# Delta rule: gated outputs and two gate slabs on ScalarE's DMA queue in place of SyncE's

## The chip, the cores and the metric

The kernel runs on one core of one Trainium2 chip. The metric is device time in microseconds, from the median of several executions; less is better. A core has five engines that run side by side: TensorE (PE, matmuls; PEld is its loading of weights), VectorE (DVE), ScalarE (ACT), GpSimd (POOL) and SyncE (SP). SP computes nothing here; it issues DMAs, one after the other. ScalarE can issue DMAs too, from the same instruction stream that holds its computing. A DMA that is issued is carried by the core's 16 DMA engines, and its end is told by a semaphore, on which whoever needs the data waits.

## What is computed

One step of a two-layer streaming encoder on 2048 prompt tokens and 32 sample tokens, width 1024, all in float32. The first layer is a gated delta rule with 8 heads of 128 x 128 state; the second is windowed attention. The change lies in the first layer:

```python
def delta_layer(x, conv_buf, s0, w_in, conv_w, a_log, dt_bias, norm_w, w_out, ln_g, ln_b):
    proj = x @ w_in
    qkv, new_buf = causal_conv(proj[..., :CONV_DIM], conv_buf, conv_w)
    z = proj[..., CONV_DIM:CONV_DIM + A_VW].reshape(b, l, A_HEADS, A_DV)
    ...
    o, s_new = gated_delta_rule(q, k, v, g, beta, s0.astype(jnp.float32))
    o = o * lax.rsqrt(jnp.mean(o * o, -1, keepdims=True) + RMS_EPS) * norm_w * jax.nn.silu(z.astype(jnp.float32))
    out = o.reshape(b, l, A_VW).astype(x.dtype) @ w_out
    return layer_norm(DN_ALPHA * x + out, ln_g, ln_b), new_buf, s_new.astype(x.dtype)
```

The delta rule itself runs in blocks: within a block all tokens are treated at once through the inverse of a triangular matrix, and a state `S` is handed from block to block, so the blocks follow each other.

## The kernel before

**Stages.** First `P1.qkv` projects q, k and v for all tokens and stores them to scratch memory in HBM. Then `P1.z` projects the gate z for three of five token blocks (416 tokens each), and the delta rule runs (`Delta.run`, line 775). The gate of the last two blocks is projected during the delta rule by `late_z` (L257), as filler between the matmuls of a chunk. When the filler is used up, at chunk 11 (`OPEN`), the output projection's weights are loaded (`OutNorm`, `load_part_weights`), and its tiles (`O1.tiles`) become the filler. After that the second layer follows.

**The gate slabs.** Each head's gate weights are a slab of 128 x 1024, 512 KB, loaded by `fetch_weights` (L44, its DMA is L46) into `w_raw`, then split into a high half by ScalarE (L53) and a low half (L54). `late_raw` (L251) picks the buffer: even heads use the pool `wp`, odd ones the pool of the late gate. `late_z` asks for the slab two heads ahead. Its results `z` go through two buffers (L266, L267) and are stored by SP (L268).

**The chunks.** A chunk is 128 tokens; there are 16 of them and one of the 32 sample tokens, `c0`. `load` (lines 504 and 506) brings `gb` (the decays, broadcast to all partitions), `k`, `q`, `v` and `z` in, each in two halves of four heads, all by SP. `v` and `z` share one tag with three buffers, so a half of `v` or `z` takes the buffer of the one three before it. In one round of `run` the work of several chunks is interleaved; for the chunk `ch` of the round these pieces matter here:

- `changes`: matmuls `vp` (L698) and ScalarE's copy of them (L700).
- `emit` of the chunk before, `last`: PE transposes its output (`otr`, L770), VectorE multiplies it into `z` (L771), SP stores `z` to the scratch tensor `g` (L772).
- `fade` (L619): VectorE multiplies q by the decays in `gb`; after it the buffer of `gb` is free.
- `lower` of the chunk two ahead: ScalarE's small copies (L538, L541), then VectorE's transpose (L543).
- `seen`: matmuls into the one bank `op` (L712, L716) and ScalarE's copy to `o` (L718), in two halves; the second half needs the bank that the copy of the first has emptied. `squares` (L744) follows on ScalarE.
- `turn_v`: PE transposes the halves of `v` (`vtr`, L583).

**Order.** PE, VectorE and ScalarE run the delta rule in the order in which the code writes it down. The order on SP and GpSimd is chosen by the program's scheduler, from its own simulated times. On every queue an instruction waits until its semaphores are reached, and what is behind it waits too.

Of the kernel before, what the change touches and what calls it, by code (L numbers as in the profile page):

```python
# [40 lines left out]
    return es.enter_context(tc.tile_pool(name=name, bufs=bufs, **kw))  # L41


def fetch_weights(nc, pool, src):  # L44
    raw = pool.tile([128, KC, 128], F32, tag="w_raw", name="w_raw", bufs=1)
    nc.sync.dma_start(raw[:], src)  # L46
    return raw


# [8 lines left out]
def split_weights(nc, pool, src, sub):  # L58

    return split_fetched(nc, pool, fetch_weights(nc, pool, src), sub)  # L60
# [30 lines left out]
def drain(gen):  # L91
    for _ in gen:
        pass


class P1:
# [131 lines left out]
    def z(self, blocks, pool, tags, ps, sub, w):  # L228

        nc = self.nc  # L230
        for h in range(8):
            self.fetched = fetch_weights(nc, self.wp, self.I["w_in"][25 + h]) if h < 7 else None
            self.next, self.sub = None, sub
            for b in blocks:
                p = ps()
                yield from project(nc, p[:, :TB], w, self.x[b])
                th = pool.tile([128, TB], F32, tag=tags[0], name="zth")
                z = pool.tile([128, TB], F32, tag=tags[1], name="z")
                nc.scalar.activation(th[:], p[:, :TB], AF.Tanh, scale=0.5)
                nc.vector.tensor_scalar(out=z[:], in0=p[:, :TB], scalar1=self.nwh[:, 0:1], scalar2=None, op0=ALU.mult)  # L240
                nc.vector.scalar_tensor_tensor(out=z[:], in0=th[:], scalar=1.0, in1=z[:], op0=ALU.add, op1=ALU.mult)
                nc.sync.dma_start(self.T["z"][h, :, b * TB:(b + 1) * TB], z[:])
                self.split()
            w = self.next
# [6 lines left out]
    def late_raw(self, pool, h):  # L251

        if h % 2 == 0:
            return fetch_weights(self.nc, self.wp, self.I["w_in"][24 + h])
        return fetch_weights(self.nc, pool, self.I["w_in"][24 + h])

    def late_z(self, pool, w, raw):  # L257

# [174 lines left out]
class Delta:  # L433
# [329 lines left out]
    def emit(self, ch):  # L763

        nc, V, T, n = self.nc, self.nc.vector, self.T, ch.n
        for q in range(2):
            z = ch.z[q]
            tr = self.pc.tile([128, 4, 128], F32, tag="sc", name="otr")
            for j in range(4):
                nc.tensor.transpose(tr[:, j, :n], ch.o[:n, q * 4 + j, :], self.G["ident"][:n, :n])  # L770
            V.tensor_tensor(out=z[:, :, :n], in0=tr[:, :, :n], in1=z[:, :, :n], op=ALU.mult)  # L771
            nc.sync.dma_start(T["g"][q * 4:q * 4 + 4, :, ch.t0:ch.t0 + n].rearrange("h p t -> p h t"), z[:, :, :n])  # L772
            yield

    def run(self, chunks, S, first, second, side, done):


        V, P = self.nc.vector, self.nc.gpsimd
        none = iter(())
        at = lambda i: chunks[i] if 0 <= i < len(chunks) else None  # L780
        gen = lambda f, c, *a: f(c, *a) if c else none

        def go(*gens):
            for g in gens:
                next(g, None)

        c0, c1, c2 = chunks[:3]
        for name in ("gb", "k", "q", "v"):
            self.load(c1, name)
        for name in ("gb", "k", "q"):  # L790
            self.load(c2, name)
        fill = first.give
        drain(self.decays(c0))
        side(False)
        fill(9.0)
        side(False)
        low = self.lower(c0)
        go(low, low)
        fill(1.0)
        k, w, g, d, low = self.turn_k(c0), self.turn_v(c0), self.inside(c0), self.decays(c1), self.lower(c1)  # L800
        for s, us in ((w, 0.6), (k, 0.6), (w, 0.6), (k, 0.6), (g, 0.6), (g, 0.6), (d, 0.0), (d, 0.0), (d, 1.2), (d, 1.2),
                      (low, 1.2), (low, 1.2)):
            go(s)
            fill(us)
        drain(self.powers(c0))
        drain(self.fade(c0))
        side(False)
        self.spread(c0)
        k, w, g = self.turn_k(c1), self.turn_v(c1), self.inside(c1)
        for s, us in ((k, 1.0), (w, 1.0), (k, 1.0), (w, 1.0), (g, 1.0), (g, 1.0)):  # L810
            go(s)
            fill(us)
        drain(self.powers(c1))
        drain(self.decays(c2))
        self.S, S = S, self.S
        e, seen = self.errors(c0), self.seen(c0)
        go(e, e, seen)
        last, z, x = None, none, self.fade(c1)
        go(x)
        for i in range(len(chunks) + 1):  # L820
            ch, nx, n2, n3 = at(i), at(i + 1), at(i + 2), at(i + 3)
            if i == self.OPEN:
                first.rest()
            more, gate = 0.0 if n2 else 1.0, 1.13 if i < self.OPEN else 0.0
            if not n2:
                fill = second.give
            vp, a, sq, t = (gen(f, c) for f, c in ((self.changes, ch), (self.advance, ch), (self.squares, ch),
                                                   (lambda c: self.chain(c, V, c.split, 31), nx)))
            low = gen(self.lower, n2)
            go(low, x, low)  # L830
            if n2:
                self.load(n2, "v", (0,))
            go(vp, vp, z, z, x, x, low, low, t)
            if n2:
                drain(self.chain(n2, P, 0, n2.split))
            if n3:
                self.load(n3, "gb")
            if last:
                done(last)
            fill(2 * more)  # L840
            go(seen, a, t, a, t)
            fill(more)
            go(sq, seen)
            if i > self.OPEN:
                side(True)
            if n2:
                self.load(n2, "v", (1,))
            if n3:
                self.load(n3, "q", (0,))
            if i == self.OPEN:  # L850
                side(None)
                side(True)
            go(a, t, a, t, seen, sq)
            side(False)
            fill(2 * more + gate)
            if i + 4 == len(chunks):
                next(second.gen)
            if i + 2 == len(chunks):
                c0.o = self.four.tile([128, 8, 128], F32, tag="gb", name="os", bufs=2)
                self.nc.sync.dma_start(c0.o[:NS], self.T["o"][:, :, :])  # L860
            if not ch:
                self.load(c0, "z")
                drain(self.emit(c0))
                done(c0)
                break
            if i == 0:
                self.save("s_delta")
                self.S = S
            k, w, g, e, v, r, o = (gen(f, c) for f, c in (
                (self.turn_k, n2), (self.turn_v, n2), (self.inside, n2), (self.errors, nx), (self.invert, nx),  # L870
                (self.norms, ch), (self.scale, ch)))
            go(e, t, t)
            drain(t)
            if nx:
                self.spread(nx)
            go(w, e)
            if n3:
                self.load(n3, "k")
            go(g)
            fill(2 * more + 2 * gate)  # L880
            d = gen(self.decays, n3)
            p = gen(self.powers, n2)
            go(v)
            fill(gate)
            go(r, r, r, g, r, r, v, r, k, r, d)
            if i > self.OPEN:
                side(True)
            if i == 14:
                side(True)
                side(True)  # L890
            go(v, r, v)
            if i:
                self.load(ch, "z")
            fill(more)
            seen = gen(self.seen, nx)
            go(w, r, p, r, seen, k, r, d, r)
            if n3:
                self.load(n3, "q", (1,))
            fill(more)
            drain(r)  # L900
            go(o)
            if not nx:
                go(o)
                fill(2.0)
            fill(more)
            go(v, o, d)
            if i + 3 == len(chunks):
                next(second.gen)
            if i:
                z = self.emit(ch)  # L910
            else:
                self.nc.sync.dma_start(self.T["o"][:, :, :], ch.o[:NS])
            x = gen(self.fade, n2)
            go(x)
            fill(more)
            last = ch if i else None
        self.save("p_delta")
# [861 lines left out]
```

## Time and profile before

| what | value |
|---|---|
| time of three runs | 2275.78, 2281.08, 2286.36 us; median 2281.08 |
| profiled execution | 2287.22 us, its span 2285.4 us |
| PE busy | 2198.2 us, 96% of the span |
| VectorE, ScalarE, GpSimd busy | 1390.5, 896.5, 838.5 us |
| bytes moved by DMA | 257.70 MB, mean 113 GB/s |
| by SP's queue (q1) | 240.45 MB, 36.6% of the DMA engines' time |
| by ScalarE's queue (q10) | 14.91 MB, 2.0% |
| delta rule's stores of `g`, first and last | at 803.7 and 1226.0 us |

In the timeline a row has the start, the duration, the engine, the line, the operation and the tiles (out<-in); a bracket at the end tells how long the engine had been idle before and what ended that. `SPq` and `ACTq` are instructions of the queue itself, which issue or wait; their duration is the time to issue, not the transfer. In the list of waits of SP's queue the numbers are total, count and longest. The chain of waits is followed back from the last instruction; a row of it with "DMA" has the time from the issue to the moment at which the waiting work went on, as far as it lies on the chain. The row of a window has its bounds and length, the busy time of PE, PEld, VectorE, ScalarE and GpSimd with counts, the granted PE clock, the DMA engines' busy share and GB/s.

### The profile page before, as it was taken

How to read it: one execution, taken by the hardware profiler on the slowest of the kernel's cores; microseconds unless marked ns; L12 is line 12 of the kernel's file. 1: busy time of each engine (PE TensorE's matmuls, PEld its weight loads, DVE VectorE, ACT ScalarE, POOL GpSimd, SP SyncE). 2: the span in 40 equal slices, each digit the busy share in tenths (PEclk: the TensorE clock that was granted, in tenths of full speed). 3: DMA queues.
4: the chain of work that ended last, by engine and by line, in shares of the span. 5: the costliest groups of instructions: out<-in, count | busy, mean ns of one | idle time of the engine just before them, and what ended most of it. 6: DMA issues, size and time to landing. Idle time of an engine off the chain costs nothing.

```text
span 2285.4 us, 36741 instructions
## 1 busy us (share of the span) xinstructions
PE 2198.2 (96%) x13810; PEld 2007.0 (88%) x13810; DVE 1390.5 (61%) x2705; ACT 896.5 (39%) x2222; POOL 838.5 (37%) x1181
## 2 busy tenths in 40 slices
PE   8999999999998999998899999999999998999997
PEld 6999999999997888898788788999999986787774
DVE  3766666834385677877768875134442248677784
ACT  4444344333233666666642212211112236444441
POOL 1412121212120677676720200024441237555563
PEclk9999999999999999998989999999999999999998
DMA  5121112232435455556726764322121285332321
GB/s 190 66 76 66 75 66 80 102 107 102 135 107 144 98 128 122 127 122 179 195 85 195 227 190 139 99 92 75 68 77 68 83 191 162 84 93 85 92 70 51
DMA packets 275041, 257.70 MB, mean 113 GB/s; under 512 B 68096, under 2 KB 246592, under 8 KB 271520
## 3 DMA queue, kind: packets, MB, share of 16 engines
q1 hardware_dynamic: 265040, 240.45, 36.6%
q10 hardware_dynamic: 9824, 14.91, 2.0%
q8 instruction: 109, 1.79, 0.3%
q14 instruction: 68, 0.56, 0.1%
HBM read 160.14 MB, written 95.53 MB: 112 GB/s over the span
## 4 chain that ended last, share of the span: by engine, by line
PE 82%; ACT 6%; DVE 5%; DMA 4%; issue 1%; SPq 1%; POOL 0%; ACTq 0%; DVEq 0%; POOLq 0%
PE ps L77 16%; PE ps L79 16%; PE ps L78 16%; PE ot L1499 3%; PE po L1082 2%; PE po L1084 2%; PE po L1083 2%; PE po L1384 2%; PE po L1385 2%; PE po L1386 2%; PE S L1478 2%; DMA v<-s_v 2%; PE tr L1493 2%; PE vp L698 1%; ACT kd L572 1%
## 5 line engine op out<-in xcount | busy, mean ns | idle before, releaser
L77 PE MATMUL ps<-act_hi,w_hi 128*128 128x416 f32 x2000 | 707.9, 354 | 10.0 <-DVE z L266 7.2
L79 PE MATMUL ps<-act_hi,w_lo 128*128 128x416 f32 x2000 | 704.7, 353 | 1.9 <-DVE w_lo L54 1.8
L78 PE MATMUL ps<-act_lo,w_hi 128*128 128x416 f32 x2000 | 702.1, 351 | 0.6 <-DVE act_lo L69 0.6
L77 PEld LDWEIGHTS ps<-act_hi,w_hi 128*128 128x128 f32 x2000 | 377.3, 189 | 15.6 <-issue 8.0
L79 PEld LDWEIGHTS ps<-act_hi,w_lo 128*128 128x128 f32 x2000 | 376.3, 188 | 6.3 <-DVE w_lo L54 2.4
L78 PEld LDWEIGHTS ps<-act_lo,w_hi 128*128 128x128 f32 x2000 | 376.7, 188 | 5.6 <-DVE act_lo L69 0.9
L54 POOL TENSOR_TENSOR w_lo<-w_raw,w_hi 128x1024 fp32r<-128x1024 f32 x55 | 144.9, 2635 | 600.7 <-ACT w_hi L53 560.3
L196 DVE SCALAR_TENSOR_TENSOR y<-R,convw,y 128x2083 f32<-128x2083 f32 x72 | 173.7, 2414 | 110.0 <-POOL convo L190 56.9
L556 POOL TENSOR_TENSOR tm<-L,Tt 128x60 f32<-128x60 f32 (+19 forms) x373 | 137.0, 367 | 143.2 <-DVE tm L556 63.0
L559 POOL TENSOR_TENSOR Tt<-Tt,tm 128x60 f32<-128x60 f32 (+19 forms) x373 | 154.6, 414 | 29.2
L1486 POOL TENSOR_TENSOR P<-P,sm 128x384 f32<-128x384 f32 (+2 forms) x128 | 100.6, 807 | 135.2 <-DVE sm L1363 82.2
L226 ACT COPY R<-ps 128x416 f32<-128x416 f32 (+1 forms) x144 | 61.2, 448 | 202.5 <-PE ps L79 177.7
L1359 ACT ACTIVATE P<-S,nm 128x192 f32<-128x192 f32 (+2 forms) x260 | 104.7, 419 | 75.9 <-DVE nm L1352 38.6
L1224 POOL TENSOR_TENSOR rs<-rs,sin 128x416 f32<-128x416 f32 x50 | 71.2, 1424 | 151.4 <-DVE rs L1223 102.0
L53 ACT CAST w_hi<-w_raw 128x1024 fp32r<-128x1024 f32 x62 | 65.0, 1048 | 148.8 <-PE ps L78 112.2
L1082 PE MATMUL po<-wo_hi,g_hi 128*128 128x512 f32 (+1 forms) x272 | 110.4, 406 | 2.9 <-DVE r L1087 2.2
L1084 PE MATMUL po<-wo_hi,g_lo 128*128 128x512 f32 (+1 forms) x272 | 106.9, 393 | 0.0
L1083 PE MATMUL po<-wo_lo,g_hi 128*128 128x512 f32 (+1 forms) x272 | 106.7, 392 | 0.0
L1499 PE MATMUL ot<-pt,vd 128*128 128x256 f32 x372 | 99.1, 392 | 6.5 <-ACT pt L1495 2.8
L1384 PE MATMUL po<-wo_hi,g_hi 128*128 128x512 f32 x240 | 99.6, 415 | 0.4 <-DVE r L1387 0.4
L1385 PE MATMUL po<-wo_lo,g_hi 128*128 128x512 f32 x240 | 97.3, 405 | 0.0
L1386 PE MATMUL po<-wo_hi,g_lo 128*128 128x512 f32 x240 | 96.5, 402 | 0.0
(284 smaller groups left out, 4039.1 us busy)
## 6 DMA issues: line engine op xcount, KB each, us to landing
w_raw<-in_w_in SPq DMA_DIRECT2D x40, 512.0 KB
w_raw<-in_b_w_in SPq DMA_DIRECT2D x20, 512.0 KB
gb<-s_gcum SPq DMA_DIRECT2D x34, 256.0 KB
k<-s_k SPq DMA_DIRECT2D x34, 256.0 KB
s_z<-z SPq DMA_DIRECT2D x40, 208.0 KB
s_bz<-za SPq DMA_DIRECT2D x40, 208.0 KB
s_bq<-ra SPq DMA_DIRECT2D x40, 208.0 KB
s_q<-y SPq DMA_DIRECT2D x8, 1024.0 KB
```

Source lines behind the costliest of these rows:

```text
L54: sub.tensor_tensor(out=lo[:], in0=raw[:], in1=hi[:], op=ALU.subtract)
L77: nc.tensor.matmul(ps, hi[:, k, :], xh[:, k, :], start=(k == 0), stop=False)
L78: nc.tensor.matmul(ps, hi[:, k, :], xl[:, k, :], start=False, stop=False)
L79: nc.tensor.matmul(ps, lo[:, k, :], xh[:, k, :], start=False, stop=(k == KC - 1))
L196: nc.vector.scalar_tensor_tensor(out=y[:], in0=R[:, j:j + W], scalar=self.convw[:, i, j:j + 1], in1=y[:], op0=ALU.mult, op1=ALU.add)
L559: P.tensor_tensor(out=Tt[:n, i0:, :w], in0=Tt[:n, i0:, :w], in1=tm[:n, i0 - k:, :w], op=ALU.subtract)
L1082: nc.tensor.matmul(ps[:n], ghi[:, k, :n], w[0][:, k, cs], start=(k == 0), stop=False)
L1083: nc.tensor.matmul(ps[:n], ghi[:, k, :n], w[1][:, k, cs], start=False, stop=False)
L1084: nc.tensor.matmul(ps[:n], glo[:, k, :n], w[0][:, k, cs], start=False, stop=(k == KC - 1))
L1384: nc.tensor.matmul(ps[:n], ghi[:, k, :n], w[0][:, k, cs], start=(k == 0), stop=False)
L1385: nc.tensor.matmul(ps[:n], ghi[:, k, :n], w[1][:, k, cs], start=False, stop=False)
L1499: nc.tensor.matmul(ot[:, p], self.vd[:, kc0 + j, p, :], pt[:, 2 * j:2 * j + 2, :], start=(j == 0), stop=(j == nj - 1))
```

## The change

The two stores of a gated chunk leave `emit` and become a method `send`, which issues them on ScalarE's queue. `run` calls it after the round's `changes`, `emit`, `fade` and `lower` pieces and before the first piece of the next chunk's triangular chain; for `c0` it is called at the end. Of the late gate slabs those of heads 2 and 3 are loaded from ScalarE's queue; the others stay on SP. What is computed and stored is the same.

```diff
-def fetch_weights(nc, pool, src):
+def fetch_weights(nc, pool, src, queue=None):
     raw = pool.tile([128, KC, 128], F32, tag="w_raw", name="w_raw", bufs=1)
-    nc.sync.dma_start(raw[:], src)
+    (queue or nc.sync).dma_start(raw[:], src)
     return raw
...
         if h % 2 == 0:
-            return fetch_weights(self.nc, self.wp, self.I["w_in"][24 + h])
-        return fetch_weights(self.nc, pool, self.I["w_in"][24 + h])
+            pool = self.wp
+        return fetch_weights(self.nc, pool, self.I["w_in"][24 + h], self.nc.scalar if h in (2, 3) else None)
...
             V.tensor_tensor(out=z[:, :, :n], in0=tr[:, :, :n], in1=z[:, :, :n], op=ALU.mult)
-            nc.sync.dma_start(T["g"][q * 4:q * 4 + 4, :, ch.t0:ch.t0 + n].rearrange("h p t -> p h t"), z[:, :, :n])
             yield
+
+    def send(self, ch):
+
+        for q in range(2):
+            dst = self.T["g"][q * 4:q * 4 + 4, :, ch.t0:ch.t0 + ch.n]
+            self.nc.scalar.dma_start(dst.rearrange("h p t -> p h t"), ch.z[q][:, :, :ch.n])
...
-            go(vp, vp, z, z, x, x, low, low, t)
+            go(vp, vp, z, z, x, x, low, low)
+            if last:
+                self.send(last)
+            go(t)
...
                 self.load(c0, "z")
                 drain(self.emit(c0))
+                self.send(c0)
                 done(c0)
```

## The prediction

> **What bounds the kernel now.** I read the page first, then the chain of waits, then the waits of SP's queue, and last the timeline of three places: one chunk in the middle of the delta rule, the chunks beside the output projection's first loads, and the start of the delta rule.
>
> ```profile
> span 2285.4 us, 36741 instructions
> PE 82%; ACT 6%; DVE 5%; DMA 4%; issue 1%; SPq 1%; POOL 0%; ACTq 0%; DVEq 0%; POOLq 0%
> ```
>
> PE carries 82% of the chain; DMA and SP's queue together carry 5%, and only they are touched. So the change can act only where PE waits for something that stands in SP's queue. SP issues in order and also stands still in order:
>
> ```profile
> SPq L772 <- DVE z L771: 94.5, 30, 8.7
> SPq L506 <- DMA s_g<-z: 11.4, 18, 3.4
> ```
>
> SP stood 94.5 us, in 30 waits, ready to store a gated output (L772) that VectorE had not finished, and 11.4 us in 18 waits for such a store to land, because `v` and `z` share three buffers and the next load goes into the buffer that the store reads. SP's standing is no loss in itself; what counts is whether anything behind it comes late. In a middle chunk it does not:
>
> ```profile
> 803.67 1.25 SPq L772 DMA_DIRECT2D s_g<-z  x2
> 803.84 0.69 DVE L771 TENSOR_TENSOR z<-otr,z 128x512 f32<-128x512 f32 x1 [0.20 <-PE otr L770]
> 804.66 0.40 ACT L541 COPY Tt<-tinit 128x256 f32<-128x256 f32 x1
> 804.97 0.58 ACT L718 COPY o<-op 128x512 f32<-128x512 f32 x1
> 805.20 0.98 SPq L504 DMA_DIRECT2D gb<-s_gcum  x2
> 806.32 1.06 PE L712 MATMUL op<-Sp,q 128*128 128x128 f32 x8
> 806.49 0.36 SPq L506 DMA_DIRECT2D v<-s_v  x1
> 808.31 0.59 ACT L718 COPY o<-op 128x512 f32<-128x512 f32 x1 [1.45 <-PE op L716]
> 821.06 0.66 PE L583 MATMUL vtr<-ident,v 128*128 128x128 f32 x4
> ```
>
> The second half of `v`, issued at 806.49, is read at 821.06 with no wait in the row. PE does wait in three chunks, once the bulk loads of the output projection share the queue:
>
> ```profile
>   DMA v<-s_v: 9.4, 3
> ```
> ```profile
> 1046.02 0.69 DVE L771 TENSOR_TENSOR z<-otr,z 128x512 f32<-128x512 f32 x1 [0.20 <-PE otr L770]
> ```
> ```profile
> 1049.06 7.04 DMA s_g<-z
> 1056.12 9.53 DMA v<-s_v
> ...
> 1080.29 14.65 DMA v<-s_v
> ...
> 1104.62 2.87 DMA s_g<-z
> 1107.56 16.23 DMA v<-s_v
> ```
> ```profile
> 1065.78 1.09 PE L583 MATMUL vtr<-ident,v 128*128 128x128 f32 x4 [2.33 <-DMA v<-s_v]
> ```
>
> The three waits are 9.4 us together, the first 2.33. In the chain rows the second column is the share that this link takes: the loads take 9.53, 14.65 and 16.23 us, the stores ahead of them at most 7.04. So the load itself is slow there, more than its release. The third place is the start:
>
> ```profile
> 686.48 0.37 SPq L46 DMA_DIRECT2D w_raw<-in_w_in  x1
> 711.33 4.80 SPq L506 DMA_DIRECT2D q<-s_q  x2
> 716.23 2.70 SPq L268 DMA_DIRECT2D s_z<-z  x1
> 719.03 0.38 SPq L46 DMA_DIRECT2D w_raw<-in_w_in  x1
> ```
> ```profile
> 701.65 0.52 ACT L283 ACTIVATE zth<-ps 128x416 f32<-128x416 f32 x1 [2.74 <-PE ps L79]
> 722.76 0.65 DVE L266 TENSOR_SCALAR z<-ps,nwh 128x416 f32<-128x416 f32 x1 [11.34 <-DMA s_z<-z]
> 723.56 0.69 PE L77 MATMUL ps<-act_hi,w_hi 128*128 128x416 f32 x1 [7.19 <-DVE z L266]
> 726.42 0.71 PE L79 MATMUL ps<-act_hi,w_lo 128*128 128x416 f32 x1 [1.83 <-DVE w_lo L54]
> ```
> ```profile
> 697.00:723.00 26.00, 19.18 (x137) 17.49 (x135) 7.58 (x17) 10.37 (x31) 0.00 (x0) 0.93 0.75 156
> ```
>
> PE stands 7.19 us for VectorE, which stands 11.34 us for a gate buffer whose store SP issued only at 716.23, behind the `q` loads; 1.83 us more go to a late weight half. The last row is the window of that stretch: DMA share 0.75, 156 GB/s.
>
> **The stores.** There are 16 pairs of 256 KB stores and one small pair. On SP one issue takes 0.36 us by its median. ScalarE's queue has issued nothing of this shape, but it has issued loads in the same place of the chunk:
>
> ```profile
> L772 SPq DMA_DIRECT2D s_g<-z x34: 359/360/1854, 803.7 to 1226.0; - x34
> L506 SPq DMA_DIRECT2D k<-s_k x36: 360/1148/6042, 598.5 to 1123.0; - x36
> ```
> ```profile
> 1079.62 0.31 ACT L744 ACTIVATE vn<-o 128x128 f32<-128x128 f32 x1
> 1079.65 0.39 ACTq L1014 DMA_DIRECT2D wo_hi<-s_wo  x1
> 1079.84 0.19 ACT L744 ACTIVATION_READ_ACCUMULATOR vn<-o 128x1 f32 x1
> 1079.93 0.29 ACT L744 ACTIVATE vn<-o 128x128 f32<-128x128 f32 x1
> 1080.09 0.47 ACTq L1015 DMA_DIRECT2D wo_lo<-s_wo  x1
> ```
>
> An issue of 0.39 us there ran while ScalarE went on computing: no idle time is marked on the rows around it. In the new place the pair stands between L541 and the copy L718. Its data is ready when ScalarE gets there: the second multiply ends at 803.84 + 0.69 = 804.53, L541 starts at 804.66. So the added wait holds ScalarE for nothing in a middle chunk; behind it in its queue stands L718, and PE waits for L718, since the one `op` bank must be emptied before L712. L718 ends at 804.97 + 0.58 = 805.55 and L712 starts at 806.32: 0.77 us of cover. The pair costs 2 x 0.39 = 0.78 if nothing of it overlaps, so 0.01 us a chunk at worst at these durations, and ScalarE's next stand of 1.45 us before the second L718 takes up the rest. Without the cover it would be 16 x 0.78 = 12.5 us. I take 0.
>
> What SP gains: 32 x 0.36 = 11.5 us of issuing, beside which nothing waits. The `gb` issue at 805.20 does not move up much, because the factor multiply that reads the old buffer follows the two multiplies on VectorE. `v` still waits for the store to land. So 0 here also.
>
> In the first crowded chunk the store was late by SP's doing: data at 1046.02 + 0.69 = 1046.71, issue at 1049.06, 2.35 us. That can give PE between 0 (the load stays behind `gb` in SP's queue) and its whole wait of 2.33 us; I take 1, nearer the lower end, since that load's own 9.53 us outweigh it. The Trainium skill (DMA: Bandwidth & Descriptors, Queues, rings and completion order) says that each DMA engine alternates between SP's and ScalarE's rings packet by packet, so the store would no longer stand behind the bulk; by it the link of 7.04 us would shrink toward the 2.87 us of the uncrowded store at 1104.62, and the sum would take the whole 2.33 us in place of 1. No row here shows a store on ScalarE's ring, so I do not go that far. In the two other crowded chunks the store is not late: 0.
>
> **The slabs.** The first moves from 686.48, where SP had room, to ScalarE's first steps of the delta rule, into that window; the second from 719.03 to just behind the row at 701.65. Both then run beside the loads of `gb`, `k` and `q` of the first two chunks. SP saves two issues of about 0.38 us, but neither stood between those loads and the store at 716.23 that PE waits for, so the gain there is 0, at most the 1.83 us of PE's second wait. The loss is that 1 MB more moves in this window ahead of that store. At 156 GB/s that is 6.7 us; the idle quarter of the DMA engines is 0.25 x 26 = 6.5 us. So between 0 and 6.7, and I take 1, because the idle share nearly holds it. ScalarE's own wait to issue the second slab has work behind it (`kd`, `vn`), but up to 7.19 us of that hides under PE's stand; uncovered, it would cost the same amount again.
>
> **Sum.** 0 - 1 + 1 = 0. The profiled execution took 2287.22 us (its span and 1.8 around it); it lies 0.3% above the median of 2281.08, within the spread of the three runs (2275.78 to 2286.36). Applied to the median: **2281 us**. The likeliest case's own range is the spread widened by the terms' bounds, 2273 to 2292.
>
> **Rival one, faster.** SP's backlog is the cause of all the stands. Then the `v` waits (9.4) and the start's (7.19 + 1.83) go: 18.4 us, 2263 us. For it: DMA and SP's queue are on the chain at just these places. Against: the slow part there is the load, and the loads stay on SP. The Trainium skill (the same page, Issuing engines are not separate DMA queues) says that spreading issues over engines saves only issue time, which would leave the `v` waits whole; the trace has no case that decides it.
>
> **Rival two, slower.** ScalarE's queue is held at the issue. On SP an issue of the same shape took 1.148 us by median (`k`), up to 6.04. With 1.148 each, a pair takes 2.30 us, 1.53 over the cover of 0.77; it decides as soon as the pair takes more than 0.77. In 13 chunks (the three crowded ones stand for `v` anyway) that is 19.9 us: 2301 us. For it: ScalarE works in the written order and feeds PE right behind the pair. Against: the two issues at 1079.65 and 1080.09.
>
> **Rival three, it does nothing.** The stores land when they did and the loads wait as before: 2281, within the first case.
>
> **Chances.** What differs by less than 0.5% (11.4 us) counts as no change, which is about what can be told here. No change 0.46; faster 0.30; slower 0.24. The range takes in both rivals' times: 2262 to 2301.
>
> **What would show it.** Right: the stores on ScalarE's queue close behind L541, the copy L718 after them no later than PE needs it, PE's `v` waits still some 9 us, and at the start still about 7 us for the gate buffer. Wrong: a new wait of PE on L718 in every chunk (rival two), or a vanished `v` wait or start stall (rival one); or SP's remaining loads standing in another order than before, which I assume they do not.

## The result and the profile after

The changed kernel takes 2286.44 us by its median (2282.05 to 2290.11), beside it the kernel before 2283.21 us (2275.78 to 2292.78). The ratio is 1.0015, with a 95% interval of 1.0004 to 1.0025: **slower by about 3.3 us**, 0.15%. This is within the half per cent that counted as no change, and inside the range, but the interval leaves out 1: the forecast of a sum of 0 was off by these 3 us. The profiled execution took 2287.71 us, its span is 2285.9 us (before 2287.22 and 2285.4).

The chain of waits of the changed kernel is nearly the old one, with PE's share two points lower and ScalarE's and SP's queue one point higher each:

```profile
PE 80%; ACT 7%; DVE 5%; DMA 4%; SPq 2%; issue 1%; POOL 0%; ACTq 0%; DVEq 0%; POOLq 0%
```

**A middle chunk**, in the timeline of the changed kernel (columns as before; lines behind the new method have numbers 6 to 9 higher), and then the matching row of the kernel before:

```profile
803.59 2.05 PE L698 MATMUL vp<-vn,u 128*128 128x128 f32 x16 [0.45 <-ACT u L678]
...
806.85 0.39 ACTq L778 DMA_DIRECT2D s_g<-z  x1
...
807.74 0.38 ACTq L778 DMA_DIRECT2D s_g<-z  x1
807.83 0.41 ACT L541 COPY Tt<-tinit 128x256 f32<-128x256 f32 x1
808.16 0.59 ACT L718 COPY o<-op 128x512 f32<-128x512 f32 x1
...
809.50 1.06 PE L712 MATMUL op<-Sp,q 128*128 128x128 f32 x8
```
```profile
800.42 2.05 PE L698 MATMUL vp<-vn,u 128*128 128x128 f32 x16 [0.45 <-ACT u L678]
```

ScalarE issues both stores, and its copy L718 starts 808.16 - 803.59 = 4.57 us after the chunk's first `vp`, as before (804.97 - 800.42 = 4.55). The pair costs nothing that shows here. The ten rounds from the second to the twelfth `vp` take as long as they did; the first two rows are of the kernel before, the next two of the changed one:

```profile
773.14 2.05 PE L698 MATMUL vp<-vn,u 128*128 128x128 f32 x16 [0.46 <-ACT u L678]
...
1042.60 2.05 PE L698 MATMUL vp<-vn,u 128*128 128x128 f32 x16 [0.45 <-ACT u L678]
```
```profile
776.29 2.05 PE L698 MATMUL vp<-vn,u 128*128 128x128 f32 x16 [0.45 <-ACT u L678]
...
1045.76 2.05 PE L698 MATMUL vp<-vn,u 128*128 128x128 f32 x16 [0.45 <-ACT u L678]
```

That is 269.46 and 269.47 us. But the changed kernel enters them 3.15 us late, and its first `vp` already starts at 745.87 in place of 742.72. **So the time is lost at the start**, ahead of the first round. (Behind 1042 us this one pair of profiles wins most of it back: the last `vp` starts at 1191.32 in place of 1190.61. Single profiles differ more than that there, as shown below; the 3.3 us are a difference of medians.) This is the start in the changed kernel:

```profile
696.38 1.02 SPq L504 DMA_DIRECT2D gb<-s_gcum  x2
696.94 0.34 ACTq L46 DMA_DIRECT2D w_raw<-in_w_in  x1
...
708.46 0.36 ACTq L46 DMA_DIRECT2D w_raw<-in_w_in  x1
708.86 1.11 ACT L572 ACTIVATE kd<-tr,t_ekd 32x128 f32<-32x128 f32 x4 [7.31 <-DMA k<-s_k]
710.02 1.04 PE L569 MATMUL tr<-ident,k 128*32 128x128 f32 x4 [3.57 <-ACT kd L572]
...
717.94 3.50 SPq L268 DMA_DIRECT2D s_z<-z  x1
...
725.57 0.65 DVE L266 TENSOR_SCALAR z<-ps,nwh 128x416 f32<-128x416 f32 x1 [9.38 <-DMA s_z<-z]
726.36 0.69 PE L77 MATMUL ps<-act_hi,w_hi 128*128 128x416 f32 x1 [4.55 <-DVE z L266]
729.23 0.71 PE L79 MATMUL ps<-act_hi,w_lo 128*128 128x416 f32 x1 [1.83 <-DVE w_lo L54]
```

Two things are new. ScalarE cannot issue the second slab before 708.46; its `kd` behind that issue is late, and PE has a new stand of 3.57 us for `kd`. And the store that frees the gate buffer is issued at 717.94 in place of 716.23, so VectorE goes on at 725.57 in place of 722.76. PE's stand for the gate buffer shrinks from 7.19 to 4.55 us, because PE comes to it late, but it ends 2.80 us later. Counted from SP's first `gb` issue, the store is issued 1.05 us later than before (717.94 - 696.38 = 21.56, before 716.23 - 695.72 = 20.51), and VectorE goes on 1.10 us later after that issue (7.63 in place of 6.53). Either the late store or the stand of ScalarE could be the cause. The window of the same stretch (columns as before):

```profile
697.00:723.00 26.00, 21.24 (x133) 18.68 (x131) 7.38 (x17) 11.69 (x37) 0.00 (x0) 0.87 0.81 172
```

DMA share 0.81 in place of 0.75, 172 GB/s in place of 156: in 26 us 16 x 26 = 416 KB more. Both slabs moved whole in this window (1.05 MB on ScalarE's queue); SP's queue moved 3.42 MB in it in place of 4.04.

**The crowded chunks.** In the chain of waits of the changed kernel:

```profile
1049.01 9.23 DMA s_g<-z
1058.25 9.27 DMA v<-s_v
...
1079.90 15.76 DMA v<-s_v
...
1108.14 2.94 DMA s_g<-z
1111.15 16.32 DMA v<-s_v
```
```profile
1048.29 0.69 DVE L771 TENSOR_TENSOR z<-otr,z 128x512 f32<-128x512 f32 x1 [0.69 <-PE otr L770]
1049.01 0.37 ACTq L778 DMA_DIRECT2D s_g<-z  x1
...
1058.25 0.36 SPq L506 DMA_DIRECT2D v<-s_v  x1
...
1067.66 1.09 PE L583 MATMUL vtr<-ident,v 128*128 128x128 f32 x4 [1.35 <-DMA v<-s_v]
```

The first store now goes out at once (ready at 1048.29 + 0.69 = 1048.98, issued at 1049.01), but its link is 9.23 us, against 7.04 before. (In the chains of e8, the same kernel, and of e1 below, it is 7.63 and 6.82 us.) PE's wait shrinks from 2.33 to 1.35 us here. The loads of `v` behind it are as slow as they were. In the second profile of the changed kernel (e8) PE stands longer in this chunk than it did before the change, so the smaller wait is not a gain of the change:

```profile
1066.99 1.09 PE L583 MATMUL vtr<-ident,v 128*128 128x128 f32 x4 [5.38 <-DMA v<-s_v]
```

### The profile page after: what moved, and what is told of

It is laid out like the page before. It is cut to its first block, busy times and chain, and to the rows that moved or that the text cites. A ratio compares the mean times of both kernels' runs of the same rounds, so it can differ in the third digit from the quotient of the medians.

```text
span 2285.9 us, 36738 instructions
## 1 busy us (share of the span) xinstructions
PE 2197.0 (96%) x13810; PEld 2005.2 (88%) x13810; DVE 1392.2 (61%) x2705; ACT 897.8 (39%) x2222; POOL 838.3 (37%) x1181
## 4 chain that ended last, share of the span: by engine, by line
PE 80%; ACT 7%; DVE 5%; DMA 4%; SPq 2%; issue 1%; POOL 0%; ACTq 0%; DVEq 0%; POOLq 0%
PE ps L77 16%; PE ps L79 16%; PE ps L78 15%; PE ot L1508 3%; PE po L1091 2%; PE po L1393 2%; PE po L1093 2%; PE po L1092 2%; PE po L1394 2%; PE po L1395 2%; PE S L1487 2%; DMA v<-s_v 2%; PE vp L698 2%; PE tr L1502 1%; ACT kd L572 1%
```

## The experiments

The theory (A): the slabs' bytes push the gate buffer's store back, and everything behind it. Its rivals: the stand of ScalarE at the issue (B), and the stores on ScalarE's queue (C). In the table, T is the time from SP's first `gb` issue of the start (L504) to the row of VectorE that waits for the gate buffer (L266): the loads and the store, without what had happened before. Each ratio is to the kernel before as it ran beside that kernel; the times of different rows are not to be compared with each other. The time of that `gb` issue differs from profile to profile, 694.80 to 698.38 us in this table, with and without the change.

| kernel | on ScalarE's queue | gb issue | T | first vp | time, us | ratio, 95% interval |
|---|---|---|---|---|---|---|
| before | nothing | 695.72 | 27.04 | 742.72 | - | - |
| e1 | stores | 695.05 | 27.63 | 742.91 | 2283.76 | 1.0003, 0.9988 to 1.0018 |
| e5 | 1/8 of slab 3 | 696.43 | 27.09 | 743.50 | 2284.85 | 1.0003, 0.9985 to 1.0021 |
| e11 | stores, in four | 698.38 | 27.35 | 746.24 | 2286.63 | 1.0018, 1.0004 to 1.0032 |
| e3 | slab 2 | 698.29 | 27.90 | 746.49 | 2286.74 | 1.0017, 1.0003 to 1.0032 |
| e4 | slab 3 | 695.25 | 28.24 | 744.87 | 2286.57 | 1.0014, 0.9999 to 1.0028 |
| e2 | slabs 2 and 3 | 697.49 | 28.76 | 746.52 | 2287.72 | 1.0019, 1.0006 to 1.0032 |
| after | stores, both slabs | 696.38 | 29.19 | 745.87 | 2286.44 | 1.0015, 1.0004 to 1.0025 |
| e8 (after, again) | stores, both slabs | 694.80 | 29.75 | 745.21 | 2288.18 | 1.0013, 0.9994 to 1.0033 |

### The two halves of the change

Stores alone (e1), slabs alone (e2), and one slab alone (e3, e4):

```diff
 e1:  late_raw of the changed kernel, with None in place of
-        self.nc.scalar if h in (2, 3) else None
 e2:  the kernel before, with fetch_weights and late_raw of the changed one
 e3:  the same with  h == 2        e4:  the same with  h == 3
```

> Only the gated outputs' stores move to ScalarE's queue; all gate slabs stay on SP. Theory A (the loss is made at the start, by the two slabs' bytes running ahead of the store of the gate buffer): no loss here, between 0 and -2.5 us against before (ratio 0.999 to 1.000); the first round of the delta rule starts (first vp, L698) where before had it, at 742.7 +- 0.5 us, and PE stands some 7.2 us for the gate buffer. Theory C (the stores on ScalarE's queue cost the time): +3 us (1.0014), and the first vp still at 742.7.

> Only the two gate slabs move to ScalarE's queue; the stores stay on SP. Theory A (slabs' bytes) and theory B (ScalarE held at the issue of the second slab) both: first vp some 3 us later than before, at 745.7 +- 0.5 us, and +3 us on the whole (1.0013), or more where the stores on ScalarE's queue won something late. Theory C (stores cost): no loss, 742.7.

> Only the slab of head 2 moves (from SP at 686 us to ScalarE at 697). Theory A: its 512 KB are half of what runs ahead of the gate buffer's store, so the store lands some 1.4 us later and the first vp starts at 744.2 (+1.5 us). Theory B (ScalarE held at the slab of head 3): nothing, 742.7.

> Only the slab of head 3 moves (from SP at 719 us, behind the gate buffer's store, to ScalarE ahead of kd). Theory A: the other half, first vp at 744.2 (+1.5 us), ScalarE's stand before kd as long as in the changed kernel (7.3 us) but hidden under PE's stand for the gate buffer. Theory B: the whole of it, first vp at 745.7 (+3 us).

The slabs alone lose as much as the change (1.0019), the stores alone nothing that can be told from zero (1.0003). By the times alone C is not excluded, since e1's interval reaches 1.0018; but e1's first `vp` is where it was, and its ten rounds take 269.6 us. One slab adds 0.6 (e3) and 1.0 us (e4) to the mean T of the four kernels without a whole slab there (27.28), both together 1.5 to 2.5. The noise of such a number is some 0.6 us: e1 and e11 change nothing before the first `vp`, and their T is 0.6 and 0.3 us above that of the kernel before. So the 0.6 of e3 is hardly clear of it.

Several numbers missed. The first `vp` of e2 and of e3 came later than expected, at 746.52 and 746.49, but there SP's loads had begun 1.77 and 2.57 us later than in the kernel before. That of e4, 744.87, lies between A (744.2) and B (745.7) and decides nothing. Counted from the `gb` issue it is 49.62 us, as late as with both slabs, and in e3 48.20. Of the 2.2 us that e4 has over the kernels without a whole slab (47.45 by their mean), only 1.0 are in T; the rest comes behind the gate buffer, where PE ran at a granted clock of 0.77 (the first row is e4, the second the kernel before, each from the row of VectorE to the first `vp`):

```profile
723.49:744.87 21.38, 18.75 (x108) 17.13 (x109) 14.98 (x24) 7.21 (x23) 0.00 (x0) 0.77 0.36 108
722.76:742.72 19.96, 17.33 (x109) 15.87 (x109) 14.98 (x24) 8.25 (x24) 0.00 (x0) 0.83 0.41 133
```

In the other kernels of the table this clock was 0.80 to 0.83. Nor do the times follow the halves: one slab alone (1.0017, 1.0014) loses as much as both, with intervals too wide to tell.

### The stand of ScalarE without the bytes

In e5 only 64 KB of the slab of head 3 are loaded from ScalarE's queue, the rest by SP behind the gate buffer's store:

```diff
+        self.nc.scalar.dma_start(raw[:, :1], self.I["w_in"][24 + h][:, :1])
+        self.nc.sync.dma_start(raw[:, 1:], self.I["w_in"][24 + h][:, 1:])
```

> Of the slab of head 3 only the first eighth (64 KB) is loaded from ScalarE's queue, at the place where the changed kernel loads all of it; the other seven eighths are loaded by SP, at the place where the kernel before loads the slab (behind the gate buffer's store). Everything else is as before. ScalarE is held at the issue just as long (some 7 us before kd), but nearly no bytes are moved ahead. Theory A (bytes): the gate buffer's store lands some 27 us after the first gb load is issued, as before (26.9), in place of 28.2 with the whole slab; the first vp starts at 742.7 +- 0.6 us, ratio 1.000. Theory B (the hold): 1.2 us later than before, as with the whole slab.

Its timeline (here lines are 5 higher than before):

```profile
708.33 0.37 ACTq L258 DMA_DIRECT2D w_raw<-in_w_in  x1
708.75 1.11 ACT L577 ACTIVATE kd<-tr,t_ekd 32x128 f32<-32x128 f32 x4 [7.13 <-DMA k<-s_k]
709.91 1.03 PE L574 MATMUL tr<-ident,k 128*32 128x128 f32 x4 [3.39 <-ACT kd L577]
...
723.52 0.65 DVE L271 TENSOR_SCALAR z<-ps,nwh 128x416 f32<-128x416 f32 x1 [7.90 <-DMA s_z<-z]
724.32 0.68 PE L77 MATMUL ps<-act_hi,w_hi 128*128 128x416 f32 x1 [3.75 <-DVE z L271]
```

The stand of ScalarE is whole (7.13 us), PE's new stand for `kd` is there (3.39 us), and it costs nothing: PE's stand for the gate buffer is shorter by as much (3.75 for 7.19), T is 27.09, and the first `vp` is 0.78 us later than before with a `gb` issue 0.71 later. So for slab 3 it is the bytes and not the hold that make the store late: T is 28.24 with the whole slab at the same place (e4). The time agrees (1.0003 against 1.0014), but the intervals overlap. For slab 2 bytes and issue were not taken apart, but its issue at 696.94 held nobody: ScalarE's next instruction, at 697.08, had no wait.

What ScalarE waits for is no data of its own. The row puts the end of its idle time to a `k` load. In the trace's semaphore events the DMAs of SP and ScalarE count on eight semaphores in turn, and an issue waits until the earlier DMA on its semaphore has landed. For the slab's issue at 708.46 in the changed kernel that was the `k` load issued by SP at 698.00 and landed at 708.38.

### The changed kernel once more

> The changed kernel once more, for a second profile. In the profiles with the slab of head 2 on ScalarE's queue, SP's first gb load was issued 0.7, 1.8 and 2.6 us later than in the kernel before, at 695.7, and in those without it 0.7 and 0.5 us earlier. If that is chance, it falls between 695.0 and 698.0 here; if it belongs to the change, it is 0.7 us late or more. From that issue to the landing of the gate buffer's store 29.1 +- 0.6 us (26.9 before). The crowded chunks behind 1042 us differ from the first profile by up to 3 us in each.

The loads began at 694.80, earlier than before, so a late start does not belong to the change. T is 29.75 with the early start, and the first `vp` 2.49 us later than before. Without a whole slab ahead, the first `vp` follows the `gb` issue by 47.00, 47.86, 47.07 and 47.86 us (before, e1, e5, e11), with both slabs by 49.49, 49.03 and 50.41 (after, e2, e8): **2.2 us more** by the means. Single pairs give 1.2 (e2 against e1) to 3.3 (e8 against e5). Of the 3.15 us by which the first profile was late there, 0.66 are its later start of the loads. The crowded part, from the twelfth to the last `vp`, took 145.6 us in the one profile of this kernel and 139.8 in the other, and 148.0 in that of the kernel before; a gain of 1 us there cannot be read from single profiles.

### Three gate buffers

If the loss comes through the store alone, a third gate buffer should take it away. In e6 the kernel before has three buffers `z`, in e7 the changed kernel, in e9 the kernel with the slabs alone; e10 has three buffers, the stores, and slab 3 alone on ScalarE's queue:

```diff
-            z = pool.tile([128, TB], F32, tag="z", name="z")
+            z = pool.tile([128, TB], F32, tag="z", name="z", bufs=3)
...
```

The tile `z` of `P1.z`, the stage before, gets `bufs=3` in the same way.

> The kernel before with three gate buffers z in place of two, so that VectorE need not wait for the store at the start. If PE's stand there (7.19 us) is all that the store costs, the first vp starts some 5 to 7 us earlier (736 to 738) and the time is 2278 +- 2 us (ratio 0.997 to 0.998); if the loads of k and q of the second chunk are the real limit there, PE stands for them in its place and it gains 0 to 3 us.

> The changed kernel with three gate buffers z in place of two. PE's stand for the gate buffer is gone, and with it the cover of ScalarE's hold at the issue of the second slab. Theory A with the hold hidden until now: the hold comes to light, the first vp is later than in the kernel before with three buffers by the 3.9 us by which ScalarE stands longer before kd (7.31 against 3.37); it gains less over the changed kernel than three buffers gain over the kernel before. If the store was the only way by which the slabs cost time, both kernels come to the same time with three buffers.

> Three gate buffers z and the two slabs on ScalarE's queue; the gated outputs' stores stay on SP. With three buffers the changed kernel came to a first vp at 737.4 us and a ratio of 0.9976, the kernel before to 741.4 and 1.000; ScalarE stood 6.73 us for the slab of head 3 in the latter and not at all in the former. If the earlier slab makes that difference: first vp at 737.4 +- 1 us, ratio 0.9975 +- 0.0015. If the stores on ScalarE's queue make it: first vp at 741, ratio 1.000.

> Three gate buffers z, the stores and the slab of head 3 on ScalarE's queue; the slab of head 2 stays on SP, at its early place at 686 us. If the slab of head 2 only adds bytes to the loads of the delta rule's start, its early place is as good or better: first vp at 736.5 to 737.4, ratio 0.997 to 0.998. If it is needed earlier than SP brings it, later than 737.4.

| kernel | three buffers and | gb issue | first vp | time, us | ratio, 95% interval |
|---|---|---|---|---|---|
| e6 | nothing on ScalarE's queue | 694.32 | 741.39 | 2284.53 | 1.0000, 0.9984 to 1.0016 |
| e7 | stores, both slabs | 694.57 | 737.45 | 2279.10 | 0.9976, 0.9961 to 0.9991 |
| e9 | both slabs | 696.41 | 741.47 | 2278.82 | 0.9968, 0.9955 to 0.9981 |
| e10 | stores, slab 3 | 694.29 | 736.76 | 2279.21 | 0.9974, 0.9961 to 0.9987 |

Both expectations for e7 failed, and this was the instructive miss. The kernel before gains nothing by a third buffer: 0 lies in the range of the second expectation for e6, but its reason, the loads of `k` and `q`, was not it. The changed kernel comes to 0.24% below the kernel before, and all three versions with slab 3 loaded early beat both kernels. ScalarE's rows of e6, the row of PE that waits for them, and then PE's rows of e7:

```profile
723.95 1.04 ACT L53 CAST w_hi<-w_raw 128x1024 fp32r<-128x1024 f32 x1 [6.73 <-DMA w_raw<-in_w_in]
724.90 1.14 ACT L572 ACTIVATE kd<-tr,t_ekd 128x128 f32<-128x128 f32 x4
```
```profile
726.09 0.66 PE L569 MATMUL tr<-ident,k 128*128 128x128 f32 x4 [2.21 <-ACT kd L572]
```
```profile
720.53 0.46 PE L77 MATMUL ps<-act_hi,w_hi 128*128 128x416 f32 x1 [0.71 <-ACT w_hi L53]
721.85 0.46 PE L79 MATMUL ps<-act_hi,w_lo 128*128 128x416 f32 x1 [0.67 <-DVE w_lo L54]
726.96 0.66 PE L583 MATMUL vtr<-ident,v 128*128 128x128 f32 x4 [0.52 <-DVE vn L585]
```

With the stand for the buffer gone, the kernel before stands at the next thing that is late: the slab of head 3, issued by SP behind that store. ScalarE waits 6.73 us to split it, and its `kd` behind. In the kernel before that wait was there too, unseen, because it ended 1.2 us after the other (723.94 against 722.76; ScalarE's row, with two buffers):

```profile
723.94 1.04 ACT L53 CAST w_hi<-w_raw 128x1024 fp32r<-128x1024 f32 x1 [6.52 <-DMA w_raw<-in_w_in]
```

So two waits lay one upon the other, for the store and for the slab. The change took away the second and lengthened the first. In e9 the uncovered stand for `kd` shows (PE's row below, 4.72 us), and its loads began 2 us later than those of e6 and e7, hence its first `vp` at 741.47, past the expected 737.4. Its ratio is in the expected range, but its start does not explain it: counted from the `gb` issue its first `vp` is only 1.9 us earlier than in the kernel before (45.06 against 47.00), and the whole is 7 us shorter. e10 came out as expected, so the early place of slab 2 on SP is as good.

```profile
712.05 1.04 PE L569 MATMUL tr<-ident,k 128*32 128x128 f32 x4 [4.72 <-ACT kd L572]
```

The stands are not the whole of the gain. These are the windows from the `gb` issue to the first `vp` in e6, e7 and e10:

```profile
694.32:741.39 47.07, 40.29 (x256) 36.61 (x255) 23.92 (x43) 20.11 (x60) 1.74 (x4) 0.93 0.60 145
694.57:737.45 42.88, 38.70 (x257) 35.05 (x255) 23.61 (x43) 20.09 (x60) 1.74 (x4) 0.96 0.69 172
694.29:736.76 42.47, 37.28 (x256) 33.95 (x254) 23.69 (x43) 20.20 (x60) 1.75 (x4) 1.00 0.65 161
```

Against e6, e7 is 4.2 us shorter and e10 4.6. Of this PE's busy time, for the same count of matmuls, makes 1.6 and 3.0 us, and the granted clock rises from 0.93 to 0.96 and 1.00; the rest is idle time of PE that is gone. The mean clock of all runs was higher too, 0.985 to 0.986 in e7, e9 and e10 against 0.983 in the kernel before beside them. Whether fewer stands bring the higher clock or it came by itself was not tested, so how much of the 0.24 to 0.32% is due to the stands stays open.

### The price of an issue, and the queue of the late store

In e11 each store goes out as two halves; in e12 the changed kernel also stores the first late head's gate buffers from ScalarE's queue:

```diff
 e11 (slabs on SP):
+        for q in range(4):
+            dst = self.T["g"][q * 2:q * 2 + 2, :, ch.t0:ch.t0 + ch.n]
...
 e12, in late_z:
-            nc.sync.dma_start(self.T["z"][h, :, b * TB:(b + 1) * TB], z[:])
+            (nc.sync if h else nc.scalar).dma_start(self.T["z"][h, :, b * TB:(b + 1) * TB], z[:])
```

> The stores on ScalarE's queue in four issues of 128 KB a chunk in place of two of 256 KB; the slabs on SP. Theory: an issue on ScalarE's queue runs beside its computing, so two more a chunk cost nothing, and a middle round stays at 26.6 and 27.9 us (the ten rounds between the second and the twelfth vp 269.5 us together). Rival: they run one after the other with its computing, then two more of 0.39 us come out from under the cover of 0.77 us: 0.78 us a chunk, ten rounds 277 us, the whole 12 us more (1.005).

> The changed kernel, with the two gate buffers of the first late head also stored from ScalarE's queue, so that VectorE's wait for the first of them no longer depends on SP, whose queue has the q loads ahead of that store. Two gate buffers as before. If the place in SP's queue is the cause of the stand: the store is issued at some 702 us in place of 717.9, lands some 5 to 8 us later, PE's stand for the gate buffer goes, the first vp starts at 737 to 739 and the ratio is 0.998. If the stores hold ScalarE longer than SP held them (each issue waits for an earlier load, as that of the slab of head 3 does until 708): kd gets later by another 3 us or more, and it gains less than 3 us.

The ten rounds of e11 took 1053.95 - 776.75 = 277.2 us, the number of the rival, but not in its way. One round took 32.6 us in place of 26.6, and the nine others only 1.6 us more together. In that round:

```profile
917.37 1.86 ACTq L778 DMA_DIRECT2D s_g<-z  x1
...
919.33 3.98 ACTq L778 DMA_DIRECT2D s_g<-z  x2
923.35 0.59 ACT L718 COPY o<-op 128x512 f32<-128x512 f32 x1 [4.99 <-issue]
...
923.99 0.38 PE L712 MATMUL op<-Sp,q 128*128 128x128 f32 x1 [4.21 <-ACT o L718]
```

Two more issues cost under 0.2 us a chunk, until two in one round are held (1.86 and 3.51 us) and L718 behind them with PE: the mechanism of rival two. This hold is not that of the slab. By the trace's semaphore events the earlier DMAs on the semaphores of these two issues had landed some 10 us before; the issues themselves took long, and why stays open. Two issues a chunk meet it lightly: in that same round one store's issue took 1.15 us in e8 and 1.13 in e1, and the round 26.7 in place of 26.6. In the first profile of the changed kernel the longest issue of a store took 0.575 us.

e12 is slower than the kernel before, 2289.22 us (ratio 1.0025, 1.0014 to 1.0037), and gains nothing on the changed kernel (1.0015, up to 1.0025), as its rival said:

```profile
710.97 0.34 ACTq L46 DMA_DIRECT2D w_raw<-in_w_in  x1
...
716.49 0.33 ACTq L268 DMA_DIRECT2D s_z<-z  x1
716.86 1.11 ACT L572 ACTIVATE kd<-tr,t_ekd 32x128 f32<-32x128 f32 x4 [14.08 <-DMA gb<-s_gcum]
...
718.02 1.04 PE L569 MATMUL tr<-ident,k 128*32 128x128 f32 x4 [9.69 <-ACT kd L572]
```

The stand for the gate buffer is gone, but ScalarE stands 14.08 us over two issues: that of the slab of head 3, and that of the second store, which waits until a `gb` load of SP has landed (at 716.41 by the semaphore events). PE stands 9.69 us for `kd`. Here the hold has no cover, and costs no less than the two stands that it replaced (4.55 + 3.57 us).

## Why the prediction was right and wrong

- **The slabs: the wrong term.** The step that failed was "between 0 and 6.7, and I take 1, because the idle share nearly holds it". The term measured 2.0 us in T (29.23 by the mean of after, e2 and e8, against 27.28) and 2.2 in the first `vp`. The mechanism, bytes ahead of the store that PE waits for, and the bounds were right; the size was not. At the 156 GB/s of the prediction the megabyte is 6.7 us. With 2.0 us lost, the idle share took in some 70% of it by this estimate, where the 1 us taken asks for 85%.
- **The stand of ScalarE at the second slab: right.** Most of it hid under PE's stand, as said. That stand is now 4.55 us for the gate buffer and 3.57 for `kd`, in place of "about 7" for the gate buffer alone. "Uncovered, it would cost the same amount again" is borne out in kind by e12 and by PE's 4.72 us of e9. The prediction gave no reason for the wait; it was for loads of SP.
- **The stores in the middle chunks: right at 0.** The copy L718 starts 4.57 us after the first `vp`, before 4.55. The rows of the weight loads at 1079.65, from which an issue beside computing was read, pointed the right way.
- **The first crowded chunk: the number agreed by luck.** PE's wait fell by 0.98 us, and 1 was taken, but in e8, with the same kernel, it was 5.38 us, and in the kernels with the stores on SP (before, e2 to e5) 0.84 to 3.01. A gain of 1 us is not shown. The delay by SP was also misread: the load of `v` waits for the first of the two stores, whose data was ready at 1045.82 (a multiply of VectorE at 1045.13, 0.69 us long), so SP was 3.2 us late and not 2.35. The `v` waits of PE, "still some 9 us", were 6.7 and 8.7 in the two profiles of the changed kernel, 5.4 in e1 and 8.3 in e2: they did not vanish. The Trainium skill (DMA: Bandwidth & Descriptors, Queues, rings and completion order) has each DMA engine alternate between the rings packet by packet. The 2.87 us to which the prediction let the store's link shrink by that rule did not come. The link was 9.23, 7.63 and 6.82 us with the store on ScalarE's ring (after, e8, e1) and 7.04 on SP's, so here the measurement speaks against reading that rule as a short way past a full queue.
- **The sum.** In place of 0 - 1 + 1 it is 0 + 2.2 at the start, and nothing that is shown from the crowded chunks. The times say +3.3, with 0.9 to 5.7 by the interval; the 2.2 lies in it, and the rest cannot be told from noise.
- **The rivals.** Rival one (SP's backlog) asked for the vanishing of the waits; moving the late store off SP (e12) removed its wait and put one of 9.69 us for `kd` in its place. Rival two's hold is real, but with the change's two issues a chunk it made one round of e8 and of e1 0.2 us longer, where rival two had 1.53 us in each of 13 chunks. "SP's remaining loads standing in another order" did not occur at the start.

## What to carry to other kernels

Before a load is moved to an earlier place, look for the transfer that ends the stand there, and count every byte put ahead of it: here the idle share of the DMA engines took up some 70% of them, and the rest was the loss. Where two waits end nearly together, removing one alone gains nothing and may cost: here the third buffer alone gave 1.0000, the early slabs alone 1.0019, and both together 0.2 to 0.3% less than before, part of it with a higher granted clock. An issue moved to a computing engine costs nothing while it goes out at once; ask what it may have to wait for, since everything behind it on that engine waits too.

## What was not expected of the hardware and the program

- An issue on ScalarE's queue waited for loads of SP through the shared semaphores. ScalarE stood 7.31 us before `kd` in the changed kernel (3.37 in the kernel before, for PE) and 14.08 us over two issues in e12. The 4.99 us in one round of e11 were of another kind: the issues themselves took long, with their semaphores free.
- The first loads of the delta rule began between 694.80 and 698.38 us over the nine profiles of the first table, 1.58 us apart in the two of one kernel (after and e8), and the first `vp` moved with them. In e11, which changes nothing before that, they began 2.66 us later than in the kernel before: more than the two slabs cost.
- A store alone on ScalarE's ring beside SP's bulk was not fast: 6.82 to 9.23 us for 256 KB in the crowded chunk, against 2.94 at 1108.14.
- PE's speed at the start differed from kernel to kernel: with the same count of matmuls, its busy time from the `gb` issue to the first `vp` was 40.29 us at a granted clock of 0.93 and 37.28 at 1.00.
